# Sliding-window attention of layer 1 by chunks: two heads of 64 queries in one tile, softmax divided before the values

## The chip, the cores and the metric

The kernel runs on one core of a Trainium2 chip. The metric is the device time of one execution in microseconds (us); smaller is better. The time before is 2668.11 us, the median of 3 runs (2667.65 to 2673.82).

The core has engines that run side by side, each working through its own instructions in order: TensorE (PE: matrix products; PEld is its loading of weights), VectorE (DVE), ScalarE (ACT), GpSimd (POOL), and SyncE (SP), which here issues the DMAs. Semaphores order them where one needs another's result. SBUF is the memory that all engines work in; PSUM is the one that TensorE writes to.

## What is computed

A two-layer encoder over 2048 prompt frames and 64 sample frames with model width 1024. Layer 0 has two kinds of attention and is not touched. Layer 1 is a grouped-query attention: 16 query heads, 2 heads of keys and values, 64 per head, in chunks of 64 frames. Each chunk reads itself and the two chunks before it, and each head has a learned sink, a logit that takes part in the softmax and has no value. Then come a SiLU gate and an output projection.

```python
def _grouped_attend(q, k, v, valid, scale, bias=None, sinks=None):
    s = jnp.einsum('...qhgd,...khd->...hgqk', q, k).astype(jnp.float32) * scale
    ...
    s = jnp.where(valid, s, NEG_INF)
    if sinks is not None:
        ...
        p = jax.nn.softmax(jnp.concatenate([s, sk], axis=-1), axis=-1)[..., :-1]
    ...
    return jnp.einsum('...hgqk,...khd->...qhgd', p.astype(v.dtype), v)

def _c_layer(h, pos, cache, pre_g, post_g, w_in, sinks, w_out):
    ...
        o = _band_prompt(q, k, v, C_PAST_CHUNKS, C_SCALE, sinks=sinks)
    ...
    return h + _rms((o * jax.nn.silu(g)) @ w_out, post_g), state
```

## The kernel before

Phases 1 to 4 make layer 0 and the input projection of layer 1, and leave queries, keys, values and gates of layer 1 in DRAM (`sQC`, `sKC`, `sVC`, `sGC`). Phase 5, the function `phase5`, is layer 1's attention with its output projection and ends the program. All numbers are kept in two parts, a high and a low one, so each product of two such matrices takes two or three matmuls.

**Units and blocks.** A block is 128 frames, 16 of them in the order 8 to 15, 0 to 7. A block has four units. Before, a unit is one group `g` of key/value heads and one parity `e` of query heads: 4 heads, each with 128 queries in the 128 rows, against 256 keys (the block's own and the block before; block 0 has 128). Two corners of 64x64 of each such tile are no part of the window; a `mask` with -1e30 in these is added to the scores.

**What a unit does.** `start` calls `score`: 8 matmuls write the scores `s` to PSUM (L1705). VectorE adds the mask and takes the maximum, one instruction for each of the 4 heads (L1708, in the trace with a small instruction that reads the maximum out), and combines it with the sink (L1709); POOL prepares the sink's exponent (L1710). `exp`: ScalarE makes the exponentials `P` in SBUF, with their sums (L1717), and POOL adds the sink's term (L1721). `turn`: for each of the two blocks of keys, 4 transposes on TensorE write `t` to PSUM (L1726), ScalarE copies the high part to `PT` (`copy`, L211) and VectorE makes the low part (`lo_of`, L214). `av`: 4 matmuls with the values into `acc` (L1733). `out`: ScalarE copies half of `acc` to `tbm`, and VectorE adds the halves into the block's output `OT` (L1823). After the fourth unit the reciprocal `ri` of all sums is taken (L1827) and `gate` is queued.

**The gate.** It loads `G`, spreads `ri` to 64 columns (`rb`, two ScalarE copies), transposes it on TensorE (L1755, 2 x 4) and multiplies `OT` by it on VectorE (L1757). Then POOL multiplies by `G` (L1763), ScalarE copies the high part of the result to `MM`, and POOL makes its low part (L1770).

**The output projection.** 16 products for a block (`products`, L964, 3 matmuls of 512 columns each) run as filling work: `pump(RATE5 / 2)` in a step issues two products or so if the credit suffices. Its results `z` go through ScalarE (copy, squares), a scaling on VectorE (L995), and an addition of the residual on POOL (L1003).

**What sets the order.** `step(n)` is one round, and three units are in work in it: exponentials of unit n+1; scores of unit n+2; transposes of n, first block of keys; products; low part of n; values and output of unit n-1; transposes of n, second block; products; low part. The first 8 rounds are ordered by a scheduler at build time. From round 8 on, TensorE, VectorE, ScalarE and SP keep the order in which the code is written. PSUM holds two `s`, two `t`, one `acc` and one product. The loads of a block's keys and queries are issued when the block two before has made its last scores, those of values a block ahead.

A sample of 64 frames goes through the same functions in the first rounds, with 2 heads of 64 queries in the 128 rows and 192 keys; it needs no mask, and uses one of zeros.

## Time and profile before

| | |
|---|---|
| runs | 2668.11 us median (2667.65 to 2673.82) |
| the profiled execution | 2665.11 us, its span from first to last instruction 2663.3 us |
| busy, of the span | PE 96%, PEld 88%, DVE 59%, ACT 52%, POOL 19% |
| TensorE clock granted | 0.992 |
| phase 5 | from about 2232 us to the end |

In the profile a line such as `L964 PE MATMUL proj<-Wo,MM` is a group of instructions: the line of the kernel, the engine, the operation, what it writes and reads by the program's names. Then come shape, count, busy time in all, the mean of one in nanoseconds, and after a second bar the engine's idle time just before them with what ended it. In the timeline a row begins with the start and the length in us and merges neighbours of one kind. L211 and L214 are the lines of the helpers `copy` and `lo_of`, so the tile's name tells what is copied. Ends of matmuls are modelled, so starts are the better measure there.

### The profile page before, as it was taken

To read this page: it belongs to the slowest core of one execution; us is meant where nothing else is said; L and a number is where in the kernel's file an instruction comes from. 1 tells how busy PE (TensorE), PEld (TensorE's weight loads), DVE (VectorE), ACT (ScalarE), POOL (GpSimd) and SP (SyncE) were. 2 spreads that over 40 slices of the span, in tenths; PEclk is the share of its full clock that TensorE was granted. 3 is DMA by queue.
4 is the path that set the end of the run, shared out by engine and by line. 5 is a ranking of instruction groups with operands and counts; after the bars stand their busy time and mean duration, and the time that the engine had idled before them with its cause. 6 is when DMAs were issued, how large, how long until landed. Compare 5 with 4: busy or idle time off the path is not lost.

```text
span 2663.3 us, 46751 instructions
## 1 busy us (share of the span) xinstructions
PE 2549.5 (96%) x16296; PEld 2330.5 (88%) x16296; DVE 1568.7 (59%) x4299; ACT 1387.5 (52%) x3548; POOL 518.9 (19%) x1110
## 2 busy tenths in 40 slices
PE   6999999999999999999899999999999999999998
PEld 6999999899998888888777888779999999688886
DVE  6553345453217878787758776565323313888996
ACT  4332242432327777777657666552233223787884
POOL 0001000001002333321200323441000100245453
PEclk9999999999999999999999999999999999999999
DMA  7546343736627666662287876766534417556652
GB/s 244 167 156 206 125 138 118 244 126 208 186 84 211 185 178 185 175 183 69 93 245 188 210 199 179 201 219 221 159 104 154 144 63 229 128 143 146 154 137 74
DMA packets 382283, 437.94 MB, mean 164 GB/s; under 512 B 49936, under 2 KB 308888, under 8 KB 378816
## 3 DMA queue, kind: packets, MB, share of 16 engines
q1 hardware_dynamic: 382048, 434.95, 55.6%
q8 instruction: 130, 2.13, 0.3%
q14 instruction: 105, 0.86, 0.1%
HBM read 282.80 MB, written 157.09 MB: 165 GB/s over the span
## 4 chain that ended last, share of the span: by engine, by line
PE 80%; DVE 8%; DMA 5%; ACT 4%; issue 2%; POOL 1%; SPq 0%; ACTq 0%; DVEq 0%; POOLq 0%
PE pm L237 39%; PE proj L964 11%; PE s L683 6%; PE acc L754 4%; PE t L726 3%; PE acc L1228 3%; PE acc L1733 2%; PE t L1203 2%; PE s L1705 2%; PE t L1726 2%; PE s L1176 2%; DVE PT L214 2%; ACT P L702 1%; DVE m L689 1%; DMA R<-in_ab_w_in_dram 1%
## 5 line engine op out<-in xcount | busy, mean ns | idle before, releaser
L237 PE MATMUL pm<-X,W 128*128 128x384 f32 (+2 forms) x4536 | 754.3, 325 | 1.7 <-DVE ev L214 1.0
L237 PEld LDWEIGHTS pm<-X,W 128*128 128x128 f32 x4536 | 732.1, 189 | 4.8 <-ACT X L211 1.4
L211 ACT ACTIVATE PT<-t 128x512 fp32r<-128x512 f32 (+3 forms) x704 | 345.0, 504 | 217.2 <-PE t L1203 74.2
L214 DVE SCALAR_TENSOR_TENSOR PT<-t,PT 128x512 fp32r<-128x512 f32 (+3 forms) x688 | 378.2, 568 | 77.1 <-ACT PT L211 74.9
L964 PE MATMUL proj<-Wo,MM 128*128 128x512 f32 (+1 forms) x1416 | 391.4, 406 | 5.9 <-ACT z L211 3.1
L214 DVE SCALAR_TENSOR_TENSOR ev<-pm,ev 128x256 fp32r<-128x256 f32 (+3 forms) x197 | 98.6, 503 | 333.2 <-ACT ev L430 98.3
L964 PEld LDWEIGHTS proj<-Wo,MM 128*128 128x128 f32 (+1 forms) x1416 | 244.4, 186 | 53.0 <-ACT z L211 6.5
L237 PE MATMUL pm<-W,X 128*128 128x256 f32 (+5 forms) x2040 | 281.1, 297 | 0.0
L237 PEld LDWEIGHTS pm<-W,X 128*128 128x128 f32 (+1 forms) x2040 | 272.0, 187 | 1.0
L702 ACT ACTIVATE P<-s,m 128x512 f32<-128x512 f32 (+9 forms) x344 | 209.3, 615 | 33.2 <-DVE m L691 30.5
L683 PE MATMUL s<-KA,Q 128*128 128x512 f32 (+7 forms) x640 | 200.3, 395 | 9.1 <-ACT P L702 8.4
L228 DVE TENSOR_TENSOR W<-R,W 128x768 fp32r<-128x768 f32 (+3 forms) x114 | 116.2, 1055 | 134.5 <-ACT W L227 134.1
L726 PE MATMUL t<-ident,P 128*128 128x128 f32 x1088 | 175.6, 275 | 3.6 <-ACT P L702 0.8
L689 DVE TENSOR_REDUCE m<-s 128x1 f32<-128x480 f32 (+7 forms) x216 | 132.5, 613 | 77.7 <-PE s L683 77.3
L726 PEld LDWEIGHTS t<-ident,P 128*128 128x128 f32 x1088 | 133.9, 140 | 41.9 <-ACT P L702 15.1
L754 PE MATMUL acc<-PT,V 128*128 128x256 f32 x1152 | 156.3, 285 | 6.5 <-DVE OT L763 6.5
L754 PEld LDWEIGHTS acc<-PT,V 128*128 128x128 f32 x1152 | 140.6, 189 | 11.9 <-PE t L726 6.0
L1717 ACT ACTIVATE P<-s,m 128x256 f32<-128x256 f32 (+2 forms) x264 | 119.1, 470 | 8.8 <-DVE m L1709 8.7
L1708 DVE CUSTOM_DVE_ANT_0 s<-s,mask 128x256 f32<-128x256 f32 (+1 forms) x256 | 107.8, 422 | 19.6 <-PE t L1726 8.5
L1228 PE MATMUL acc<-PT,V 128*128 128x256 f32 x672 | 111.5, 298 | 6.7 <-DVE OT L1238 4.5
L683 PE MATMUL s<-KR,Q 128*128 128x384 f32 (+6 forms) x320 | 115.9, 362 | 0.8 <-DMA Q<-sQR 0.8
L1180 DVE CUSTOM_DVE_ANT_0 s<-s,bias 128x640 f32<-128x640 f32 (+4 forms) x128 | 95.2, 744 | 34.2 <-PE s L1176 28.8
(251 smaller groups left out, 3928.8 us busy)
## 6 DMA issues: line engine op xcount, KB each, us to landing
Q<-sQA SPq DMA_DIRECT2D x128, 128.0 KB, 3.2
sWO<-W SPq DMA_DIRECT2D x32, 512.0 KB, 3.9
Q<-sQB SPq DMA_DIRECT2D x128, 128.0 KB, 3.4
Wo<-sWO SPq DMA_DIRECT2D x16, 1024.0 KB, 9.1
Q<-sQC SPq DMA_DIRECT2D x32, 512.0 KB, 7.9
R<-in_ab_w_in_dram SPq DMA_DIRECT2D x40, 384.0 KB, 4.2
K<-sKB SPq DMA_DIRECT2D x56, 256.0 KB, 5.5
V<-sVB SPq DMA_DIRECT2D x24, 512.0 KB, 6.5
```

The lines of the kernel that those rows point to most:

```text
L211: nc.scalar.activation(out, in_, AF.Copy)
L214: nc.vector.scalar_tensor_tensor(out, x, scale, hi, op0=ALU.mult, op1=ALU.subtract)
L228: nc.vector.tensor_tensor(Wv[:, 1, k0:k1], Rv, Wv[:, 0, k0:k1], op=ALU.subtract)
L237: nc.tensor.matmul(ps, lhs(x, k), rhs(y, k), start=(j == 0), stop=(j == n - 1))
L683: nc.tensor.matmul(s[:r, :n], self.Q[:, x, self.qo:self.qo + r], rhs, start=(x == 0), stop=(x == 2))
L689: nc.vector.tensor_reduce(m[:r, j:j + 1], s[:r, :n], axis=AX.X, op=ALU.max)
L702: nc.scalar.activation(self.P[:r, o0:o0 + n], self.s.pop(j)[:r, :n], AF.Exp, bias=self.m[:r, 6:7], accum_out=acc)
L726: nc.tensor.transpose(t[:, b], self.P[:, (b0 + b) * 128:(b0 + b + 1) * 128], ident)
L754: nc.tensor.matmul(acc[:, (i // 2) % 2], H.V[:, b0 + b], PT[:, x, b], start=(b0 + b == 0 and x == 0), stop=(b0 + b == i and x == 1))
L964: nc.tensor.matmul(p, M[:, x, k, :r], W[k][:, y, cs], start=(k == k0 and t == 0), stop=(k == k1 - 1 and t == 2))
L1228: nc.tensor.matmul(acc, self.H.V[:, self.base - self.H.b0 + b], self.PT[:, x, off + b], start=(b == 0 and x == 0), stop=(b == nblk - 1 and ...
L1717: nc.scalar.activation(self.P[:, c, :w], self.s[:, c, :w], AF.Exp, bias=m[:, 1, c:c + 1], accum_out=m[:, 0, c:c + 1])
```

## The change

A unit becomes one chunk `ch` of 64 queries and one group `g`: 8 heads, as 4 tiles of two heads with 64 queries each, against exactly the 192 keys of the window. The mask goes. The maximum of all four tiles is taken by one instruction. The exponentials are divided by their sums (`divide`) before they are transposed, and the gate's transposed reciprocals go. Keys start at a multiple of 64, so the second chunk of a block needs a shifted piece of values, `VH`; queries are loaded by chunk.

```diff
-                def score(self, lhs, widths, mk, w, snk, nsnk, rsum):
-                    self.w, self.snk, self.rsum = w, snk, rsum
+                def score(self, lhs, widths, w, g):
...
-                    for c in range(4):
-                        nc.vector.tensor_tensor_reduce(s[:, c, :w], s[:, c, :w], mk, 1.0, -3e38, ALU.add, ALU.max, m[:, 0, c:c + 1])
-                    nc.vector.scalar_tensor_tensor(m[:, 1], m[:, 0], -1.0, nsnk, op0=ALU.mult, op1=ALU.min)
-                    nc.gpsimd.tensor_tensor(m[:, 2], m[:, 1], snk, op=ALU.add)
+                    nc.vector.tensor_reduce(m[:, 0], s[:, :, :w], axis=AX.X, op=ALU.max)
+                    nc.vector.scalar_tensor_tensor(m[:, 1], m[:, 0], -1.0, nssink[:, js], op0=ALU.mult, op1=ALU.min)
+                    nc.vector.tensor_tensor(m[:, 2], m[:, 1], ssink[:, js], op=ALU.add)
...
-                        nc.gpsimd.tensor_tensor(self.rsum, m[:, 0], m[:, 2], op=ALU.add)
+
+                def divide(self):
+                    m, w = self.m, self.w
+                    nc.vector.tensor_tensor(m[:, 0], m[:, 0], m[:, 2], op=ALU.add)
+                    nc.vector.reciprocal(m[:, 0], m[:, 0])
+                    nc.vector.tensor_tensor(self.P[:, :, :w], self.P[:, :, :w], m[:, 0, :, None].to_broadcast([128, 4, w]),
+                                            op=ALU.mult)
...
-            def gate(OT, ri, t0, r):
+            def gate(OT, t0, r):
...
-                        copy(rb, ri[:, g].rearrange("p e c -> p c e")[:, :, :, None].to_broadcast([128, 4, 2, 64]))
...
-                for _ in range(YRB if r == 128 else YRS):
-                    yield
...
-                        nc.tensor.transpose(tv[:, j], rbs[g][:, j].rearrange("p e d -> p (e d)"), ident)
-                    if r == 128:
-                        nc.vector.tensor_tensor(OT[:, js], OT[:, js], tv, op=ALU.mult)
...
-                    yield
+                yield
+                yield
                 nc.gpsimd.tensor_tensor(OT[:, :, :r], OT[:, :, :r], G[:, :, :r], op=ALU.mult)
...
-                    for x in range(2):
-                        dma(f(self.Q[x * 64:x * 64 + 64]), sQC[x][:, :, t0:t0 + 128].rearrange("h d t -> d h t"))
+                    for ch in range(2):
+                        for x in range(2):
+                            dma(f(self.Q[x * 64:x * 64 + 64, ch]),
+                                sQC[x][:, :, t0 + ch * 64:t0 + ch * 64 + 64].rearrange("h d t -> d h t"))
...
+                    if i:
+                        self.VH = vc.tile([64, 2, 128], F32R, name="VH")
+                        dma(f(self.VH).rearrange("p g x -> p (g x)"), sVC[self.lo * 128 + 64:self.lo * 128 + 128])
...
+                    k0, w = (ch * 64, 192) if B.i else (0, ch * 64 + 64)
...
+                def parts(self):
+
+                    B, ch, g = self.B, self.ch, self.g
+                    if not B.i:
+                        return [(0, 64 + ch * 64, B.VC[:64 + ch * 64, 0, g])]
+                    if ch:
+                        return [(64, 128, B.VC[:, 1, g]), (0, 64, B.VH[:, g])]
+                    return [(0, 128, B.VC[:, 0, g]), (128, 64, B.VC[:64, 1, g])]
...
-                    nc.vector.tensor_tensor(B.OT[e * 64:e * 64 + 64, g * 4:g * 4 + 4].rearrange("p j q -> p (j q)"),
-                                            self.acc[0:64], tbm, op=ALU.add)
...
+                    for e in range(2):
+                        nc.vector.tensor_tensor(B.OT[e * 64:e * 64 + 64, g * 4:g * 4 + 4, ch * 64:ch * 64 + 64],
+                                                av[:, :, e], tv[:, :, e], op=ALU.add)
...
                     if b == 0 and prv:
                         prv.av()
                         prv.out()
+                if nxt:
+                    nxt.divide()
```

How this stands on the engines in the loop, in the built programs. First VectorE before, from the end of one unit's maxima to the start of the next unit's: `m` are the small statistics, `PT` the low parts of the transposed exponentials, `OT` the output adds, and the row L1757 is the gate's.

```order
L1708 ISA m 128x1
L1709 SCALAR_TENSOR_TENSOR m<-m,nsink 128x4
L214 SCALAR_TENSOR_TENSOR PT<-t,PT 128x512
L1823 TENSOR_TENSOR OT<-acc,tbm 64x512
L1827 RECIPROCAL ri<-rsum 128x16
L214 SCALAR_TENSOR_TENSOR PT<-t,PT 128x512
L1757 TENSOR_TENSOR OT<-OT,t 128x512
L1708 ISA s,m<-s,mask 128x256
```

VectorE in the changed program, one round.

```order
L1699 TENSOR_REDUCE m<-s 128x4
L1700 SCALAR_TENSOR_TENSOR m<-m,nssink 128x4
L1701 TENSOR_TENSOR m<-m,ssink 128x4
L214 SCALAR_TENSOR_TENSOR PT<-t,PT 128x512
L1814 TENSOR_TENSOR OT<-acc,tbm 64x4x64 x2
L214 SCALAR_TENSOR_TENSOR PT<-t,PT 64x512
L1715 TENSOR_TENSOR m<-m 128x4
L1716 RECIPROCAL m<-m 128x4
L1717 TENSOR_TENSOR P<-P,m 128x768
```

The round now ends with the division of unit n+1 (L1715 to L1717), behind the output adds of unit n-1 and the second low part of unit n. On TensorE before, two rounds of a block, from the transposes of a unit on (`rb` is the gate's):

```order
L1726 MATMUL t<-ident,P 128x128 x4
L964 MATMUL proj<-Wo_24640,MM 128x512 x3
L964 MATMUL proj<-Wo_24996,MM 128x512 x3
L964 MATMUL proj<-Wo_25872,MM 128x512 x3
L1733 MATMUL acc<-PT,VC 128x512 x4
L1726 MATMUL t<-ident,P 128x128 x4
L964 MATMUL proj<-Wo_25874,MM 128x512 x3
L964 MATMUL proj<-Wo_25876,MM 128x512 x3
L1755 MATMUL t<-ident,rb 128x128 x4
L1705 MATMUL s<-KC,Q 128x256 x8
L1726 MATMUL t<-ident,P 128x128 x4
```

And in the changed program, where a block's four rounds have 9, 6, 9 and 6 products between the first transposes and the values:

```order
L1723 MATMUL t<-ident,P 128x128 x4
L964 MATMUL proj<-Wo_24640,MM 128x512 x3
L964 MATMUL proj<-Wo_24996,MM 128x512 x3
L964 MATMUL proj<-Wo_25866,MM 128x512 x3
L1730 MATMUL acc<-PT,VC 128x512 x4
L964 MATMUL proj<-Wo_25868,MM 128x512 x3
L1723 MATMUL t<-ident,P 64x128 x4
L964 MATMUL proj<-Wo_25870,MM 128x512 x3
L964 MATMUL proj<-Wo_26284,MM 128x512 x3
L1697 MATMUL s<-KC,Q 128x192 x8
L1723 MATMUL t<-ident,P 128x128 x4
```

The gate's transposes are gone, the scores have 192 columns, and the second transposes give 64 rows; the scores of unit n+2 still stand ahead of the first transposes of unit n.

## The prediction

> **What bounds the kernel now.** I read the windows view first, to see which stage the edited code is in and what is full there, then the groups of TensorE in that stage, then one round of its loop in the timeline. The edited code runs from about 2232 us to the end. Columns of the first view: window, length, busy time (and count) of PE, PEld, DVE, ACT, POOL, granted clock, DMA share, GB/s.

> ```profile
> 2225.00:2300.00 75.00, 65.06 (x411) 54.02 (x410) 47.87 (x163) 45.09 (x148) 9.13 (x32) 0.98 0.72 209
> 2320.00:2610.00 290.00, 287.26 (x1689) 247.57 (x1688) 258.62 (x687) 234.42 (x711) 142.29 (x318) 1.00 0.55 136
> 2615.00:2664.00 49.00, 36.35 (x165) 28.59 (x163) 27.02 (x60) 13.23 (x27) 17.05 (x18) 0.92 0.26 86
> ```
> ```profile
> L964 PE MATMUL proj<-Wo,MM 128*128 128x512 f32 x608 | 164.4, 406 | 0.0
> L1705 PE MATMUL s<-KC,Q 128*128 128x256 f32 x368 | 54.1, 290 | 0.0
> L1733 PE MATMUL acc<-PT,VC 128*128 128x512 f32 x192 | 52.6, 394 | 2.4 <-DVE OT L1823 2.4
> ```

> In the loop's 290 us TensorE is idle for 2.7 us, and its costliest groups waited 2.4 us for another engine: TensorE is the bound. VectorE, at 258.6 us (89%), is the next. Now one round, from one `t` (first transpose group of a unit) to the next:

> ```profile
> 2482.44 0.60 PE L1726 MATMUL t<-ident,P 128*128 128x128 f32 x4
> 2482.80 1.62 PE L964 MATMUL proj<-Wo,MM 128*128 128x512 f32 x6
> 2484.26 1.08 PE L1733 MATMUL acc<-PT,VC 128*128 128x512 f32 x4
> 2485.18 0.60 PE L1726 MATMUL t<-ident,P 128*128 128x128 f32 x4
> 2485.44 0.59 ACT L211 ACTIVATE tbm<-acc 64x512 f32<-64x512 f32 x1 [1.76 <-PE acc L1733]
> 2485.53 0.94 PE L964 MATMUL proj<-Wo,MM 128*128 128x512 f32 x3
> 2486.07 0.69 DVE L1823 TENSOR_TENSOR OT<-acc,tbm 64x512 f32<-64x512 f32 x1 [0.56 <-ACT tbm L211]
> 2486.31 0.60 PE L1755 MATMUL t<-ident,rb 128*128 128x128 f32 x4
> 2486.66 1.20 PE L1705 MATMUL s<-KC,Q 128*128 128x256 f32 x8
> 2486.76 0.25 DVE L1827 RECIPROCAL ri<-rsum 128x16 f32<-128x16 f32 x1
> 2486.93 0.63 DVE L214 SCALAR_TENSOR_TENSOR PT<-t,PT 128x512 fp32r<-128x512 f32 x1
> 2487.70 0.60 PE L1726 MATMUL t<-ident,P 128*128 128x128 f32 x4
> 2488.05 2.36 PE L964 MATMUL proj<-Wo,MM 128*128 128x512 f32 x9
> 2490.25 1.09 PE L1733 MATMUL acc<-PT,VC 128*128 128x512 f32 x4
> ...
> 2602.30 0.25 DVE L1827 RECIPROCAL ri<-rsum 128x16 f32<-128x16 f32 x1
> ```

> Starts of TensorE's groups follow each other without a hole, so differences of starts are prices: 4 transposes 0.36, 6 products 1.46, 9 products 2.20, 3 products 0.78, 4 value matmuls 0.92, 8 scores of 256 columns 1.04. The reciprocal comes once a block; its rows at 2486.76 and 2602.30 are five blocks apart, so **a block of four units takes 23.1 us**. The transposes of a unit never wait long: its exponentials were done a round before. That is the slack the change spends.

> **What the change removes and adds on VectorE.**

> ```profile
> L1708 DVE CUSTOM_DVE_ANT_0 s<-s,mask 128x256 f32<-128x256 f32 x240 | 103.0, 431 | 19.0 <-PE t L1726 8.5 <-PE s L1705 4.8
> L1708 DVE DVE_READ_ACCUMULATOR2_ANT m<- 128x1 f32 x264 | 37.0, 140 | 0.1
> L1757 DVE TENSOR_TENSOR OT<-OT,t 128x512 f32<-128x512 f32 x32 | 21.6, 678 | 3.5 <-PE t L1755 3.3
> L689 DVE TENSOR_REDUCE m<-s 128x1 f32<-128x512 f32 x48 | 33.1, 689 | 20.1 <-PE s L683 19.9
> L689 DVE TENSOR_REDUCE m<-s 128x1 f32<-128x384 f32 x24 | 13.3, 554 | 6.9 <-PE s L683 6.7
> L1238 DVE TENSOR_TENSOR OT<-acc,tbm 64x256 f32<-64x256 f32 x16 | 6.7, 416 | 10.1 <-ACT tbm L211 9.8
> L228 DVE TENSOR_TENSOR W<-R,W 128x768 fp32r<-128x768 f32 x70 | 64.7, 964 | 39.4 <-ACT W L227 39.1
> 2267.97 0.20 DVE L1863 RECIPROCAL ris<-rss 128x8 f32<-128x8 f32 x1 [2.16 <-POOL rss L1721]
> ```

> Removed per unit: four mask-and-maximum pairs, 4 x (0.43 + 0.14) = 2.28 us, and a quarter of the gate's two multiplications and reciprocal, (2 x 0.68 + 0.25) / 4 = 0.40. Added: one reduction of 768 scores, 0.69 + 256 x (0.689 - 0.554) / 128 = 0.96; a small add taken over from POOL, 0.2; two output adds of 64x256 for one of 64x512, 2 x 0.416 - 0.69 = 0.14; and the division: a small add and a reciprocal, 0.20 each, and a multiplication of 768 with 768, 0.96 by the L228 row, 1.36 together. That is 2.68 out and 2.66 in: VectorE's load stays. **Its place in the order does not.** The division of unit n+1 stands behind the output adds of unit n-1 and the second low part of unit n, and the first transposes of unit n+1 now wait for it (both are in the rows of the built order above). So a round becomes a closed loop: transposes of n, products, values of n-1, `tbm` on ScalarE, output adds, low part, division, transposes of n+1.

> Length of that loop with 6 products between transposes and values: start of `t` to start of the output add, 2486.07 - 2482.44 = 3.63; output adds 0.83; low part 0.63; division 1.36; one hop to TensorE 0.10 (as from the end of `acc`, 2484.26 + 1.08, to `tbm` at 2485.44). Sum 6.55. With 9 products the values start 2490.25 - 2487.70 = 2.55 after `t` in place of 1.82: 7.28. The new order has 9, 6, 9, 6 in a block: 2 x (6.55 + 7.28) = **27.7 us a block**. The products behind the values, the second transposes and the scores (0.8 to 3.4 us a round) lie beside the loop and no longer count.

> TensorE's own work shrinks: a block loses the two groups L1755, 2 x 0.35 = 0.7, and scores of 192 columns cost between 4 transposes' rate (0.09 each) and today's 0.13, say 0.11: 8 x 0.02 = 0.16 a unit. 23.1 - 0.7 - 0.6 = 21.8 a block, so it would idle about 6 us of 27.7. Those savings are worth nothing here, as it is not the bound any more. The second transposes have 64 columns of weights; I count no gain (0 to 0.2 us a unit, also beside the loop).

> Fourteen blocks run in the fixed order (units 8 to 63). Thirteen pay 27.7 - 23.1 = 4.6: 60 us. Block 0 has one part of keys and no second low part (no 0.63, two value matmuls fewer): about 2. **Sum +62.**

> **POOL.** The division's multiplication reads both operands from SBUF, and so does L995.

> ```profile
> L995 DVE SCALAR_TENSOR_TENSOR z<-z,rs,g_post 64x512 f32<-64x512 f32 x4 | 2.9, 732 | 0.0
> 2491.18 3.59 DVE L995 SCALAR_TENSOR_TENSOR z<-z,rs,g_post 128x512 f32<-128x512 f32 x2
> 2491.81 2.42 POOL L1770 TENSOR_TENSOR MM<-OT,MM 128x1024 fp32r<-128x1024 f32 x1 [0.86 <-ACT MM L211]
> L1763 POOL TENSOR_TENSOR OT<-OT,G 128x1024 f32<-128x1024 f32 x13 | 31.7, 2441 | 38.3 <-DVE OT L1757 38.3
> ```

> Alone it takes 0.73; two of them took 3.59 while POOL's `MM` of 2.42 ran, 2.1 more than 1.46: nearly all of POOL's time. POOL has three such instructions a block. That on `x` starts behind the second L995, which stands right behind a division, and misses the next one. For the other two, with phases taken as random in a round of 6.9 us, a division that begins inside waits 1.2 on average (2.4 of 6.9), one caught before its multiplication waits the whole 2.4 (0.4 of 6.9), one caught within it perhaps 1.2 (0.96 of 6.9): 0.72 each, 1.45 a block, **+20** for 14 blocks. Bounds: 0 if they never meet, 2 x 2.4 x 14 = 67 if they always do. [...]

> **The first eight units** stand in an order of the scheduler's own. There TensorE is idle for 10 of 75 us already and VectorE's load is unchanged; each unit's transposes stand one division later, 8 x 1.36 = 11 at worst, and the sample's gate loses its transposes and copies, perhaps 6. I take +3 (-6 to +11).

> **The end.**

> ```profile
> 2621.45 0.68 DVE L1823 TENSOR_TENSOR OT<-acc,tbm 64x512 f32<-64x512 f32 x1 [2.25 <-ACT tbm L211]
> 2627.49 1.13 ACT L211 ACTIVATE rb<-ri 128x512 f32<-128x512 f32 x2
> 2631.18 2.42 POOL L1763 TENSOR_TENSOR OT<-OT,G 128x1024 f32<-128x1024 f32 x1
> ```

> Between the last output add and POOL's gate lie 9 us of reciprocal, `rb` copies, transposes and multiplications, which go. TensorE has other products meanwhile, so I count 4 groups of transposes at 0.36 and about 1.5 of its waiting: -3 (0 to -8).

> **Loads.**

> ```profile
> Q<-sQC SPq DMA_DIRECT2D x22, 512.0 KB, 7.4
> ```

> The queries come in twice the DMAs with half-size packets, and each block brings one small load more. They are issued over a block (23 us) ahead of their first use and land in 7.4; even twice that is hidden by the block in hand. If it were not, a block would wait some 2 us for its issue, 28 in all; I count 0. ScalarE (234 of 290 busy) loses two `rb` copies a block and a quarter of each exponential; POOL loses two small instructions a unit. Neither sets the loop, so 0.

> **Sum:** 62 + 20 + 3 - 3 = +82. The profiled execution took 2665.1 (span 2663.3); it lies 0.1% under the median shown, 2668.1. **Forecast 2747 us.**

> **Rivals.** (1) *TensorE stays the bound.* If the division were ready before TensorE comes round, a block would cost TensorE's own 21.8: 2665 - 14 x 1.3 - 3 = 2644, faster. It decides as soon as the loop is below 5.4 a round, so some 1.4 us must go from it: the whole division. For it speaks TensorE's 99% now; against it the order, in which nothing on VectorE can pass. Chance 0.09. (2) *The loop closes, but is shorter than my rows*, for example because the multiplication by a value repeated along a row reads only one full operand and meets neither 0.96 nor POOL: with 0.5 for the division a block is 4 x 0.86 = 3.4 shorter, 2665 + 62 - 13 x 3.4 = 2683. Chance 0.07 for this and what lies between it and no change, of which 0.03 within 0.3%. (3) *The loop without POOL*: 2665 + 62 = 2727. Chance 0.2. (4) *POOL and the division always meet*, since both follow the output adds: 2665 + 62 + 67 = 2794. Chance 0.12.

> **How the numbers follow.** Forecast with an average POOL term 0.52; rivals (1) to (4) 0.09, 0.07, 0.2, 0.12. Range: from the loop with no POOL and the low ends of first units and tail, 2665 + 62 - 6 - 8 = 2713, less 0.15 us of error in each of 52 rounds, 2705, up to (4), 2795. That leaves out (1), (2) and a little at the upper end, under 0.2. Faster by over 0.3% (8 us, about what a measurement of this kernel can tell from no change): 0.09, rival (1); within: 0.03; slower: the rest, 0.88.

> **What would show it.** In the new profile, between 2320 and 2610: TensorE 75 to 82% busy in place of 99%; its idle time before the first transposes, released by the `P` multiplication (L1717) and over 1 us a round; blocks 27 to 30 us apart; VectorE's busy time per block unchanged within 10% unless POOL stretches L1717, whose mean then is 1.0 to 1.6 us against 0.96. A TensorE that stays 97% busy would make the forecast wrong, and rival (1) right. A mean of L1717 near 0.5 would speak for (2).

## The result, and the profile after

The changed kernel takes 2803.34 us (median of 4 runs, 2799.87 to 2803.59) beside 2667.88 for the kernel before in the same measurement: ratio 1.0494, 95% interval 1.0479 to 1.0508. The profiled execution has a span of 2798.1 us against 2663.3 before, 134.8 longer; the forecast was 82 longer.

Windows of the changed kernel, with the columns of the first view of the prediction:

```profile
2225.00:2300.00 75.00, 66.49 (x371) 53.66 (x369) 45.50 (x100) 38.56 (x133) 7.32 (x4) 0.86 0.83 211
2320.00:2610.00 290.00, 229.49 (x1131) 175.95 (x1132) 193.55 (x396) 152.57 (x498) 85.35 (x152) 0.92 0.53 108
```

TensorE is busy for 229.5 of 290 us, 79% in place of 99%, and VectorE for 67% in place of 89%: no engine is full. And the granted clock of TensorE, 1.00 before, has a mean of 0.92; ahead of the loop, in the first row, it is 0.86 where it was 0.98. To place the loss, the values of unit 8 (the first unit of the order that is written out) and of unit 63 (the last) serve as marks, first before and then after:

```profile
2306.37 0.86 PE L1733 MATMUL acc<-PT,VC 128*128 128x512 f32 x3
...
2619.69 1.09 PE L1733 MATMUL acc<-PT,VC 128*128 128x512 f32 x4
```
```profile
2316.22 1.05 PE L1730 MATMUL acc<-PT,VC 128*128 128x512 f32 x3
...
2757.06 0.63 PE L1730 MATMUL acc<-PT,VC 128*128 128x512 f32 x2
```

The stretch to unit 8 is 9.8 us longer (forecast 3), **the loop from there to unit 63 takes 440.8 us in place of 313.3, 127.5 more (forecast 82)**, and what follows is 2.6 shorter (41.0 against 43.6; forecast 3). The three make the 134.8. So the miss lies in the loop. Its waits between 2320 and 2610 (who waited for whom: us in all, times, longest):

```profile
PE t L1723 <- DVE P L1717: 58.1, 35, 4.3
...
DVE OT L1814 <- POOL MM L1745: 21.7, 8, 3.3
```

The first row is the wait that the prediction named: TensorE at a unit's first transposes, for the division, 1.7 us a time. The second was in no term: the output adds stand still for POOL's `MM`, which holds the output buffer of two blocks before. One long round in the timeline:

```profile
2574.84 0.63 PE L1723 MATMUL t<-ident,P 128*128 128x128 f32 x4 [0.81 <-DVE P L1717]
...
2576.70 1.29 PE L1730 MATMUL acc<-PT,VC 128*128 128x512 f32 x4
...
2578.02 2.36 POOL L1738 TENSOR_TENSOR OT<-OT,G 128x1024 f32<-128x1024 f32 x1 [6.18 <-DMA G<-sGC]
...
2578.66 0.85 DVE L1814 TENSOR_TENSOR OT<-acc,tbm 64x256 f32<-64x256 f32 x2 [1.43 <-ACT tbm L211]
...
2579.52 0.68 DVE L214 SCALAR_TENSOR_TENSOR PT<-t,PT 64x512 fp32r<-64x512 f32 x1
...
2580.34 2.34 POOL L1003 TENSOR_TENSOR x<-z,x 128x1024 f32<-128x1024 f32 x1
...
2580.65 2.85 DVE L1717 TENSOR_TENSOR P<-P,m 128x768 f32<-128x768 f32 x1
...
2583.65 1.09 PE L1723 MATMUL t<-ident,P 128*128 128x128 f32 x4 [4.22 <-DVE P L1717]
2584.39 2.05 PE L964 MATMUL proj<-Wo,MM 128*128 128x512 f32 x4
```

The order is the forecast's: transposes, values, output adds, low part, division, transposes. But POOL's residual add on `x` began 0.3 us ahead of the multiplication, which took 2.85 us in place of 0.96 (the prediction had held `x` harmless), the round took 8.81 us with 6 products (forecast 6.55 and a mean of 0.4 for POOL), and after a stall of 4.22 us four products took 2.05 us at a granted clock of 0.50 (2581.80 to 2588.62): the nine of this round took 3.98 us from start to start, nine before the change 2.20. That slow stretch was not in the prediction at all.

VectorE's groups between 2320 and 2610 show where POOL hits:

```profile
L1717 DVE TENSOR_TENSOR P<-P,m 128x768 f32<-128x768 f32 x33 | 35.4, 1074 | 1.1
...
L1715 DVE TENSOR_TENSOR m<-m 128x4 f32<-128x4 f32 x36 | 13.7, 380 | 0.1
L995 DVE SCALAR_TENSOR_TENSOR z<-z,rs,g_post 128x512 f32<-128x512 f32 x16 | 11.9, 743 | 0.0
L1700 DVE SCALAR_TENSOR_TENSOR m<-m,nssink 128x4 f32<-128x4 f32 x37 | 10.0, 272 | 1.3
L1701 DVE TENSOR_TENSOR m<-m,ssink 128x4 f32<-128x4 f32 x36 | 8.0, 223 | 1.2
```

Instructions on four numbers a row take 0.22 to 0.38 us in the mean; with POOL idle they take 0.15 to 0.16 (rows of `e6_early_idle` below). They read two operands from SBUF too, and are stopped as the wide one is: in this window 14 instructions of L1717, L1715, L1700 and L1701 ran long (L1717 up to 2.90 us, L1715 2.21, L1700 1.58, L1701 2.36), and beside each of the 14 one of POOL's three wide ones was at work. L995 met one here for 0.08 us at most (0.743 in the mean, as with POOL idle), and the reciprocal L1716, which has one operand, took 0.18 us both times that it ran wholly beside POOL.

### The profile page after: what moved, and what is told of

Read it like the earlier page. It is cut to its first block, busy times and chain, and to the rows that moved or that the text cites. A ratio compares the mean times of both kernels' runs of the same rounds, so it can differ in the third digit from the quotient of the medians.

```text
span 2798.1 us, 46250 instructions
## 1 busy us (share of the span) xinstructions
PE 2593.0 (93%) x16160; PEld 2330.2 (83%) x16160; DVE 1583.9 (57%) x4111; ACT 1360.8 (49%) x3516; POOL 494.3 (18%) x970
## 3 DMA queue, kind: packets, MB, share of 16 engines
q1 hardware_dynamic: 416528, 435.93, 54.4%
## 4 chain that ended last, share of the span: by engine, by line
PE 72%; DVE 13%; ACT 6%; DMA 5%; issue 2%; POOL 1%; SPq 0%; ACTq 0%; DVEq 0%; POOLq 0%
PE pm L237 36%; PE proj L964 9%; PE s L683 5%; PE acc L754 4%; PE t L726 3%; DVE PT L214 3%; PE acc L1228 2%; DVE P L1717 2%; PE acc L1730 2%; PE s L1176 2%; PE t L1203 2%; PE t L1723 2%; DVE OT L1814 2%; ACT tbm L211 1%; DVE m L689 1%
## 5 line engine op out<-in xcount | busy, mean ns | idle before, releaser
L211 ACT ACTIVATE PT<-t 128x512 fp32r<-128x512 f32 (+3 forms) x704 | 344.8, 503 | 293.0 <-PE t L1723 97.8
L214 DVE SCALAR_TENSOR_TENSOR PT<-t,PT 128x512 fp32r<-128x512 f32 (+4 forms) x688 | 378.8, 569 | 80.6 <-ACT PT L211 77.5
L964 PE MATMUL proj<-Wo,MM 128*128 128x512 f32 (+1 forms) x1416 | 415.2, 426 | 3.5 <-ACT z L211 3.1
L964 PEld LDWEIGHTS proj<-Wo,MM 128*128 128x128 f32 (+1 forms) x1416 | 260.0, 197 | 59.9 <-issue 7.8
L214 DVE SCALAR_TENSOR_TENSOR ev<-pm,ev 128x256 fp32r<-128x256 f32 (+3 forms) x197 | 98.6, 503 | 333.5 <-ACT ev L430 97.4
L702 ACT ACTIVATE P<-s,m 128x512 f32<-128x512 f32 (+9 forms) x344 | 209.5, 616 | 33.1 <-DVE m L691 30.5
L683 PE MATMUL s<-KA,Q 128*128 128x512 f32 (+7 forms) x640 | 201.2, 396 | 9.3 <-ACT P L702 8.4
L228 DVE TENSOR_TENSOR W<-R,W 128x768 fp32r<-128x768 f32 (+3 forms) x114 | 116.3, 1055 | 134.3 <-ACT W L227 133.9
L689 DVE TENSOR_REDUCE m<-s 128x1 f32<-128x480 f32 (+7 forms) x216 | 132.4, 613 | 79.9 <-PE s L683 79.4
L1723 PE MATMUL t<-ident,P 128*128 128x128 f32 (+1 forms) x512 | 87.2, 298 | 96.0 <-DVE P L1717 92.5
L726 PEld LDWEIGHTS t<-ident,P 128*128 128x128 f32 x1088 | 134.5, 141 | 41.9 <-ACT P L702 15.1
L754 PE MATMUL acc<-PT,V 128*128 128x256 f32 x1152 | 156.0, 285 | 6.3 <-DVE OT L763 6.3
L1723 PEld LDWEIGHTS t<-ident,P 128*128 128x128 f32 (+1 forms) x512 | 55.9, 135 | 124.6 <-issue 91.5
L211 ACT ACTIVATE tbm<-acc 64x512 f32<-64x512 f32 (+1 forms) x136 | 77.5, 570 | 154.7 <-PE acc L1730 124.5
L754 PEld LDWEIGHTS acc<-PT,V 128*128 128x128 f32 x1152 | 140.4, 188 | 11.5 <-PE t L726 6.0
L1814 DVE TENSOR_TENSOR OT<-acc,tbm 64x256 f32<-64x256 f32 x128 | 53.3, 416 | 122.7 <-ACT tbm L211 92.5
L683 PE MATMUL s<-KR,Q 128*128 128x384 f32 (+6 forms) x320 | 116.3, 363 | 1.7 <-DMA Q<-sQR 1.7
## 6 DMA issues: line engine op xcount, KB each, us to landing
sWO<-W SPq DMA_DIRECT2D x32, 512.0 KB, 3.8
V<-sVB SPq DMA_DIRECT2D x24, 512.0 KB, 6.5
```

The source lines that it names most:

```text
L211: nc.scalar.activation(out, in_, AF.Copy)
L214: nc.vector.scalar_tensor_tensor(out, x, scale, hi, op0=ALU.mult, op1=ALU.subtract)
L228: nc.vector.tensor_tensor(Wv[:, 1, k0:k1], Rv, Wv[:, 0, k0:k1], op=ALU.subtract)
L683: nc.tensor.matmul(s[:r, :n], self.Q[:, x, self.qo:self.qo + r], rhs, start=(x == 0), stop=(x == 2))
L689: nc.vector.tensor_reduce(m[:r, j:j + 1], s[:r, :n], axis=AX.X, op=ALU.max)
L702: nc.scalar.activation(self.P[:r, o0:o0 + n], self.s.pop(j)[:r, :n], AF.Exp, bias=self.m[:r, 6:7], accum_out=acc)
```

## The experiments

The kernels are made from the changed one except where said. "Loop" is the time between the two marks, 55 rounds; those of before and after are 313.3 and 440.8. `e1`, `e9` and `e12` are medians of 4 runs, `e8` of 10, the others single runs. `e2`, `e3`, `e5` and `e6` leave work out, so their output is not the layer's: they only price an order. The loop of `e11` has the changed kernel's instructions and is 5.0 longer, so a difference of a few us between single loops tells nothing.

| kernel | us | loop | clock, 2320 to 2610 |
|---|---|---|---|
| e1_early | 2734.4 | 375.5 | 0.92 |
| e2_no_mult | 2676.9 | 319.8 | 1.00 |
| e3_pool_idle | 2758.9 | 401.0 | 0.96 |
| e4_fill | 2781.7 | 415.0 | 0.98 |
| e5_idle_fill | 2752.4 | 390.3 | 1.00 |
| e6_early_idle | 2673.7 | 314.5 | 1.00 |
| e7_early_act | 2790.6 | 430.9 | 0.89 |
| e8_before_chunks | 2672.5 | 314.5 | 0.99 |
| e9_early_dve | 2737.4 | 373.6 | 0.95 |
| e10_ot3 | 2794.3 | 432.4 | 0.92 |
| e11_ev3 | 2809.5 | 445.8 | 0.92 |
| e12_spread | 2743.5 | 377.0 | 0.95 |

### Is it the place of the division? e1, e2, e6

```diff
+                    if b == 0 and nxt:
+                        nxt.divide()
                     if b == 0 and prv:
                         prv.av()
                         prv.out()
-                if nxt:
-                    nxt.divide()
```

> The three instructions of the division of unit n+1 stand behind the first low part of unit n in VectorE's order, ahead of the output adds of unit n-1, in place of behind the second low part; every other engine keeps its order and no work changes. Theory A (the place of the division in VectorE's order closes the loop): a round has TensorE's other products, values and second transposes beside the division again, TensorE is the bound or nearly, its granted clock stays at 1.0, and blocks are 22 to 25 us apart: 2803 - 14 x 9 to 11.5 = 2640 to 2680 us. Rival B (the amount of work on VectorE and its collisions with POOL set the round, wherever the division stands): 2760 us or more, blocks over 30 us.

Measured: 2734.36 us (2729.48 to 2740.9), ratio to before 1.0234 (1.0209 to 1.0259). The same work in another place is 69 us faster than the change, but half of the loss stays: the time lies between the two that were expected. Windows and VectorE's groups of `e1_early`:

```profile
2320.00:2610.00 290.00, 259.22 (x1328) 201.12 (x1326) 252.85 (x462) 177.87 (x582) 112.27 (x185) 0.92 0.62 127
```
```profile
L1717 DVE TENSOR_TENSOR P<-P,m 128x768 f32<-128x768 f32 x39 | 43.8, 1122 | 1.3
...
L995 DVE SCALAR_TENSOR_TENSOR z<-z,rs,g_post 128x512 f32<-128x512 f32 x18 | 32.7, 1817 | 0.0
...
L1700 DVE SCALAR_TENSOR_TENSOR m<-m,nssink 128x4 f32<-128x4 f32 x42 | 25.4, 604 | 1.4
L1715 DVE TENSOR_TENSOR m<-m 128x4 f32<-128x4 f32 x42 | 10.5, 249 | 0.0
```

VectorE is now busy for 87%, and a good part of that is standing still. Against the means with POOL idle (next kernel), L995 lost 18 x (1.817 - 0.740) = 19.4 us, L1700 42 x (0.604 - 0.163) = 18.5, L1717 39 x (1.122 - 0.962) = 6.2, L1715 42 x (0.249 - 0.152) = 4.1: 48 of 290 us. The output adds' waits for `MM` are not the reason here: they are 2.3 us in this window. What shows it is the same order without POOL's three wide instructions:

```diff
-                nc.gpsimd.tensor_tensor(OT[:, :, :r], OT[:, :, :r], G[:, :, :r], op=ALU.mult)
...
-                nc.gpsimd.tensor_tensor(MM[:, 1, :, :r], OT[:, :, :r], MM[:, 0, :, :r], op=ALU.subtract)
+                copy(MM[:, 1, :, :r], OT[:, :, :r])
...
-            nc.gpsimd.tensor_tensor(res[:r], z[:r], res[:r], op=ALU.add)
```

(The last line goes in phase 5 alone, where `z` is stored in place of the sum.)

> The division early as in e1_early, and POOL's three wide instructions taken off as in e3_pool_idle, both; the output is not the reference's. If e1 stays at 2734 because VectorE stands still some 2 us at each of POOL's three instructions and is then full, VectorE has 20 to 21 us of work a block here, TensorE is the bound as in e2_no_mult (22.9 us a block) and the time is 2660 to 2685 us. Rival F (in e1 something else in the new order holds the rounds, for example the exponentials of a unit that now must be done half a round sooner): 2705 us or more, blocks over 25 us.

Measured: 2673.66 us. Windows and groups of `e6_early_idle`:

```profile
2320.00:2610.00 290.00, 287.75 (x1578) 223.54 (x1575) 241.50 (x550) 220.47 (x702) 42.89 (x182) 1.00 0.67 145
```
```profile
L1720 DVE TENSOR_TENSOR P<-P,m 128x768 f32<-128x768 f32 x46 | 44.2, 962 | 1.6
...
L995 DVE SCALAR_TENSOR_TENSOR z<-z,rs,g_post 128x512 f32<-128x512 f32 x22 | 16.3, 740 | 0.0
...
L1703 DVE SCALAR_TENSOR_TENSOR m<-m,nssink 128x4 f32<-128x4 f32 x51 | 8.3, 163 | 1.7
L1704 DVE TENSOR_TENSOR m<-m,ssink 128x4 f32<-128x4 f32 x51 | 8.3, 162 | 1.8
L1718 DVE TENSOR_TENSOR m<-m 128x4 f32<-128x4 f32 x50 | 7.6, 152 | 0.0
```

(Lines are 3 higher in this file.) TensorE is full again. The same with the division in its old place (`e3`) has a loop of 401.0, so the place alone is worth 86.5 us when POOL is idle. From the other side, the multiplication left out where it stands:

```diff
-                    nc.vector.tensor_tensor(self.P[:, :, :w], self.P[:, :, :w], m[:, 0, :, None].to_broadcast([128, 4, w]),
-                                            op=ALU.mult)
```

> Leaves out the multiplication of the probabilities by the reciprocal sums (the add and the reciprocal stay where they are), so the output is not divided. Theory A with collisions (C): the round loses the multiplication, 1.05 us by its mean, and with it the waits for POOL, 2.3 us a block, and the half clock, 2.2 us a block: 33.6 - 4.2 - 2.3 - 2.2 = 24.9 us a block, 2803 - 14 x 8.7 = 2681 us. If the collisions and the clock have other causes, only 4.2 go: 2745 us. Rival B: VectorE loses one eighth of its work, and the time falls by the same 4.2 a block or less, 2745 us or more, with VectorE near full.

Measured: 2676.91 us. TensorE in `e2_no_mult`, in which VectorE and POOL still meet:

```profile
2320.00:2610.00 290.00, 283.18 (x1548) 219.13 (x1547) 224.50 (x491) 205.36 (x675) 121.92 (x216) 1.00 0.68 142
```

With nothing written to `P` on VectorE, the transposes wait for ScalarE alone, whose exponentials are done a round before: the loop is open, and TensorE is busy for 98%. The multiplication is one instruction of 1.07 us in the mean, 64 of them are 69 us; without it the kernel is 126 us faster. Rival B, the amount of work, falls. The output adds still wait 29.1 us for `MM` in this window, and VectorE's 491 instructions take 224.5 us, where in `e6` the 504 beside the multiplications take 197.3; but with the loop open neither holds TensorE.

### POOL and the clock: e3, e4, e5

`e3_pool_idle` has the three edits of `e6` on POOL's work, with the division in its old place:

> Takes the three instructions of 128x1024 off POOL in the last stage: leaves out the gate's multiplication and the residual add, and makes the second half of MM a copy on ScalarE in place of a subtraction on POOL; the output is not the reference's. Theory C (VectorE's two-input multiplication stands still beside POOL, and output adds wait for POOL's MM) : 2.3 + 1.0 us a block go, 30.3 us a block, 2757 us; if the half clock follows from the long stalls that POOL causes, it goes too: 28 us a block, 2725 us, the forecast's loop without POOL. Rival: POOL's part is a story and the loop itself is 33 us long: 2790 us or more.

Measured: 2758.94 us, loop 401.0, 39.8 less. That is what theory C named without the clock (2757); the half clock went only in part (mean 0.96 in place of 0.92). One of its rounds, the check on the sum of the prediction without POOL (L1726 are the transposes, L1733 the values, L1816 the output adds, L1718 to L1720 the division):

```profile
2406.97 0.63 PE L1726 MATMUL t<-ident,P 128*128 128x128 f32 x4 [0.50 <-DVE P L1720]
...
2408.82 1.29 PE L1733 MATMUL acc<-PT,VC 128*128 128x512 f32 x4
2409.38 0.29 PEld L1733 LDWEIGHTS acc<-PT,VC 64*128 64x128 f32 x2 [0.36 <-issue]
...
2410.77 0.85 DVE L1816 TENSOR_TENSOR OT<-acc,tbm 64x256 f32<-64x256 f32 x2 [1.43 <-ACT tbm L211]
...
2411.64 0.68 DVE L214 SCALAR_TENSOR_TENSOR PT<-t,PT 64x512 fp32r<-64x512 f32 x1
...
2412.64 0.96 DVE L1720 TENSOR_TENSOR P<-P,m 128x768 f32<-128x768 f32 x1
...
2413.74 0.52 PE L1726 MATMUL t<-ident,P 128*128 128x128 f32 x3 [2.20 <-DVE P L1720]
```

From `t` to the output adds 3.80 (forecast 3.63), adds 0.87 (0.83), low part and the two small instructions 1.00 with the multiplication 0.96 (0.63 + 1.36), hop 0.14 (0.10): 6.77 against 6.55.

The clock: four products that wait for nothing, set into TensorE's stall.

```diff
                     t = ps_t.tile([128, 512], F32, name="t")
+                    for _ in range(4 if fill else 0):
+                        nc.tensor.matmul(t, fill.KC[:, 0, 0, :128], fill.Q[:, 0, :8]..., start=True, stop=True)
```

> Adds four products of 128x512, about 1 us, ahead of each unit's first transposes on TensorE, into the same PSUM tile, which the transposes then overwrite; they wait for nothing and lie in TensorE's stall. Theory D (a stall of 2 to 4 us drops the granted clock to half for 3.4 or 6.8 us in each block, and that costs 2 to 2.5 us): with the stalls 1 us shorter the granted clock stays at 1.0 in most blocks, and the time falls by up to 14 x 2.3 = 32, to about 2770 us, though TensorE has 56 us more to do. Rival E (the half clock is not a matter of the stall's length, or costs nothing): 2803 us or up to 20 more.

Measured: 2781.67 us: 21.7 faster than the change, with 4 more matmuls a unit. Windows of `e4_fill`:

```profile
2320.00:2610.00 290.00, 264.28 (x1357) 199.47 (x1356) 208.66 (x422) 161.36 (x528) 92.21 (x156) 0.98 0.55 116
```

The mean clock rose from 0.92 to 0.98, not to 1.00, and the gain fell short of the 32 that were the most. Both edits together:

> POOL's three wide instructions taken off as in e3_pool_idle, and the four products ahead of the first transposes as in e4_fill, both; the output is not the reference's. e3 showed rounds of 6.8 and 7.4 us at full clock, 28.3 us a block, and a half clock for 3.4 us in most blocks. Theory D (the half clock follows from the stalls): it goes, the blocks are 28.3 us or less, and the time is 10 to 15 us below e3's 2759: about 2745 us, 18 above the 2727 that the loop without POOL was forecast at. Rival E (filling a stall gains nothing once POOL is idle): 2759 us or more.

Measured: 2752.40 us, clock 1.00, loop 390.3, 10.7 less than `e3` has. The whole time fell by 6.5 us, less than the 10 to 15 that were expected, and it is a single run beside a single run; what carries theory D is `e4`, where added work speeds the kernel up as the clock rises. In the loop, idling POOL is worth 39.8, filling the stalls 25.8, both together 50.5: 15.1 are common to them. That fits `e3`, where the clock rose from 0.92 to 0.96 as POOL's stops went.

### Other prices: e7, e8, e10, e11

`e7_early_act` divides early and with four scaled copies of 128x192 on ScalarE:

```diff
+                    for c in range(4):
+                        nc.scalar.activation(self.P[:, c, :w], self.P[:, c, :w], AF.Copy, scale=m[:, 0, c:c + 1])
```

> The division early, and its multiplication as four scaled copies of 128x192 on ScalarE in place of one on VectorE: VectorE loses 3.8 us a block, ScalarE gains 4 x 4 x 0.41 = 6.6 and then has about 23.6 us a block. If VectorE with its stops for POOL is what holds e1, this is faster than e1: ScalarE and TensorE share the bound at 23 to 24.5 us a block, 2680 to 2710 us. If ScalarE's order makes a new closed loop (exponentials, scaled copies, copies of the next transposes): 2734 us or more.

Measured: 2790.58 us, so the rival holds. From the waits of `e7_early_act` (L1718 is the scaled copy):

```profile
ACT P L1718 <- DVE m L1716: 81.6, 37, 7.5
```

ScalarE waits 2.2 us a time at its own copies for the reciprocal, with all its other work of the round behind them: a closed loop again, now through ScalarE's order.

`e8_before_chunks`, the kernel before with the queries in four DMAs a block:

```diff
-                    for x in range(2):
-                        dma(f(self.Q[x * 64:x * 64 + 64]), sQC[x][:, :, t0:t0 + 128]...)
+                    for ch in range(0, 128, 64):
+                        for x in range(2):
+                            dma(f(self.Q[x * 64:x * 64 + 64, :, ch:ch + 64]), sQC[x][:, :, t0 + ch:t0 + ch + 64]...)
```

> The kernel before, with nothing changed but its loads of queries: four DMAs a block with packets of half the size in place of two, as the change has them. The prediction counted 0 for the loads: 2668 us, ratio 1.000 within 0.003. If they are behind the 9.8 us that the first eight units lost (the DMA queues are 0.84 to 0.91 busy there), 2674 to 2680 us.

Measured: ratio 1.0004 (0.9993 to 1.0015). The 0 for the loads of queries was right.

`e10_ot3` has a third output buffer (`bufs=3` for `OT` in place of 2):

> The changed kernel with a third OT buffer, so that a block's first output add doesn't wait for POOL's MM of two blocks before; TensorE, VectorE and ScalarE keep their order. In the changed kernel VectorE's output adds waited 27 us for POOL's MM between 2320 and 2700, 10 times. If these waits lie in the closed loop, they go, about 2 us in most blocks: 2775 to 2790 us. Rival: what releases them is the order of POOL's and ScalarE's work, the wait falls on the next instruction, 2797 us or more.

Measured: 2794.31 us, between the two expectations; the loop is 8.4 shorter, little more than the 5.0 by which two loops of the same instructions differ. The output adds wait for `MM` no more, but half of the 21.7 us came back as their waits for `tbm` (65.3 us between 2320 and 2610, 54.4 in the changed kernel).

`e11_ev3`, more buffers for the stores at the start of the stage (`pool("ev5", 4)` in place of 2):

> The changed kernel with four buffers in place of two for the tiles from which the queries are stored at the start of the stage. ScalarE waited 13.3 us for these stores there, and with it the exponentials; the values of unit 8 began at 2316.2 us, 9.8 later than before the change. Theory G (these waits are what the first eight units lost beyond the division): the values of unit 8 begin at 2309 to 2313 and the time is 3 to 7 us less, 2796 to 2800 us. Rival: the order that the scheduler made has the loss in other places, 2315 to 2318 again.

Measured: 2809.49 us, the values of unit 8 at 2320.9: no gain. A miss.

### POOL's work on VectorE: e9, e12

```diff
-                yield
-                yield
-                nc.gpsimd.tensor_tensor(OT[:, :, :r], OT[:, :, :r], G[:, :, :r], op=ALU.mult)
+                for _ in range(5):
+                    yield
+                nc.vector.tensor_tensor(OT[:, :, :r], OT[:, :, :r], G[:, :, :r], op=ALU.mult)
...
+                yield
-                nc.gpsimd.tensor_tensor(MM[:, 1, :, :r], OT[:, :, :r], MM[:, 0, :, :r], op=ALU.subtract)
+                nc.vector.tensor_tensor(MM[:, 1, :, :r], OT[:, :, :r], MM[:, 0, :, :r], op=ALU.subtract)
```

> The division early, and POOL's three wide instructions of the last stage done by VectorE: the gate's multiplication (five side steps after its load in place of two), the second half of MM (one side step after its first half) and the residual add. VectorE's own work in e6_early_idle was 241.5 of 290 us, 18.7 a block of 22.5; with three instructions of 128x1024 at 1.15 to 1.3 us it is 22.4 a block, beside TensorE's 22.5. Theory C (each of them on POOL stops VectorE for some 2 us, longer than VectorE needs to do it): faster than e1_early's 2734, 2675 to 2710 us. Rival: VectorE's stops in e1 were not POOL's, and more work on VectorE makes it slower than 2734.

Measured: 2737.37 us (ratio 1.0259, 1.023 to 1.0289), no better than `e1`; 2675 to 2710 was a miss. TensorE in `e9_early_dve`, once a block:

```profile
2403.26 3.71 PE L964 MATMUL proj<-Wo,MM 128*128 128x512 f32 x15
```

Fifteen products in a row: the later gate meets the code's rule that no more than two blocks are open, and `out` then issues the rest of the gate and products in one lump, VectorE's gate work among it. `e12_spread` put two more steps into the gate:

> e9_early_dve with the gate's three steps apart: two side steps between its multiplication and the first half of MM, one more before the second half. In e9 VectorE had 20.2 us of work a block, not more than TensorE's 22.5, but ScalarE waited 5 us in each block at the first half of MM for the multiplication, which stood behind z and x on VectorE, and TensorE lost it in that round. If that is the reason for e9's 2737, these waits go and the blocks come to 23 to 24 us: 2685 to 2710 us. Rival: VectorE's work done in lumps of 3 to 4 us holds the unit's own chain wherever it stands: 2730 us or more.

Measured: 2743.49 us, a miss too. Its ScalarE still waited 43.6 us, 10 times, for the gate's multiplication (49.2 in `e9`). The lump stayed, so neither kernel tells what POOL's work would cost on VectorE if it were spread, nor refutes the rival of `e12` that such lumps hold the unit wherever they stand. That stays open.

## Why the prediction was wrong in size

**The mechanism was right.** The division's place in VectorE's order closed the loop; TensorE fell to 79% (75 to 82 were named), its first transposes wait 1.7 us a round for L1717 (over 1), and opening the loop takes the loss away without the multiplication (`e2`) or with POOL idle (`e6`), and half of it with all the work there (`e1`). Blocks are 32.1 us apart (440.8 / 55 rounds, times 4), where 27 to 30 were named. VectorE's busy time a block stayed: 89% of 23.1 us is 20.6, 67% of 32.1 is 21.4.

**The loop without POOL, +62, was 77 at most** (`e5`: 390.3 - 313.3, with the fill in it). The terms were each a little short, 0.22 us in the round shown. The largest part, 0.17 between `t` and the output adds, is the values: with 128 rows and then 64, their four matmuls hold TensorE longer (below).

**The step that failed: the sum has no term for the clock, and "POOL +20" was too small.** With the loop at 77, POOL and the clock are the other 50.5 (`after` less `e5`), where the sum had 20. Filling the stalls, which brought back most of the clock, is worth 25.8 (`e4`); the sum put the clock at nothing, without a reason. The other 24.7 (`e4` less `e5`) go with POOL; without the fill POOL is worth 39.8 (`e3`). By these differences, of the 45.5 us by which the loop was missed about 15 lie in the round itself, 5 in POOL and 26 in the clock.

Within POOL's term, the division lost about what was forecast: by the means above, 33 x 0.112 + 36 x 0.228 = 11.9 us in 290, 1.3 a block against 1.45, though `x`, held harmless, was among what it met. What the prediction did not let POOL do came beside it: L1700 and L1701 lost 37 x 0.109 + 36 x 0.061 = 6.2 us, and the output adds wait 21.7 us for POOL's `MM`. How much of either lengthens the round is not shown: L1700 and L1701 stand ahead of output adds that wait for `tbm` in any case, and without the waits for `MM` the loop was 8.4 shorter (`e10`), in a single run. Rival (4), POOL meeting every division, came within 9 us of the time by luck: of 37 multiplications in this window two ran long beside POOL, and it too has no term for the clock.

**TensorE's own block of 21.8 us was wrong.** In `e6`, where TensorE is full, two first transposes a block apart:

```profile
2406.09 0.60 PE L1726 MATMUL t<-ident,P 128*128 128x128 f32 x4
...
2408.63 1.29 PE L1733 MATMUL acc<-PT,VC 128*128 128x512 f32 x4
2409.84 0.98 PE L964 MATMUL proj<-Wo,MM 128*128 128x512 f32 x3
...
2429.48 0.60 PE L1726 MATMUL t<-ident,P 128*128 128x128 f32 x4
```

23.4 us, not less than the 23.1 before. The scores became cheaper as estimated (0.87 from start to start against 1.04), but the four values cost 1.21 in place of 0.92. So rival (1) at 2644 could not be had: with the loop open this change gives 2674 to 2677, with work left out, no gain on before. No kernel here beats the one before.

**The first eight units, +3, were +9.8.** Neither the multiplication (`e2`: unit 8 at 2314.3) nor POOL (`e6`: 2316.4) nor the loads (`e8`, before with chunks: 2308.2 against 2306.4) accounts for it, and more buffers did not help (`e11`). The scheduler makes another order there; which part of it costs the 8 us stays open. One candidate is the clock: from 2225 us to unit 8, the record has 23.9 us at half clock, 3.4 before. But `e8`, with a mean clock of 0.89 from 2225 to 2300 us (0.86 in the changed kernel), reached unit 8 only 1.8 later, so that is not shown. **The end, -3, was -2.6.**

## What to carry to other kernels

When a step moves from an engine that was done early to an in-order engine that also serves the previous unit, add up the loop from one unit's start to the next by each engine's order; here 1 us of work a unit, on an engine with room, cost 126 us, clock and POOL's part included. Then ask what the stalls of that loop do to the clock of the engine that waits (here a mean of 0.92 in place of 1.00), and count the small instructions with two SBUF operands among those that meet POOL's wide ones: here some of 0.15 to 0.16 us took up to 2.36 beside them. Price a cheaper shape on the full engine by start-to-start times with its neighbours of another shape, not by its own row.

## What the hardware showed that was not expected

**The clock.** Its record in the trace changes in steps of 3.41 us. Three such windows of the changed kernel, around a stall of 2.19 us:

```profile
2387.25:2390.66 3.41, 3.41 (x20) 2.42 (x18) 1.35 (x4) 1.20 (x3) 2.33 (x1) 1.00 0.70 195
2390.66:2394.07 3.41, 1.22 (x12) 1.07 (x11) 3.31 (x7) 2.77 (x11) 0.06 (x1) 1.00 0.34 136
2394.07:2397.49 3.42, 3.42 (x10) 2.68 (x9) 1.29 (x4) 1.21 (x3) 0.39 (x2) 0.50 0.00 0
```

**A change of rows between matmuls.** In the round of `e3` above, TensorE's loading of weights is idle for 0.36 us, waiting for nothing that the profile shows, ahead of the weights of 64 rows that follow those of 128 rows, and for 0.37 us where weights of 128 rows follow. The four values take 1.21 us from start to start, 0.3 more than four of 128 rows before; 60 units have such values. In the changed kernel the wait ahead of the weights of 64 rows came 34 times between 2320 and 2610, 12.9 us in all. What TensorE does in it, no run shows. The prediction had counted the split of 192 keys into 128 and 64 as free.
